# Strassen parts of both feed-forwards: fixed order of TensorE's products, and another order of the downs and of a chunk's last unit

## The chip, the cores and the metric

The kernel runs on one core of a Trainium2 chip. Five engines matter, each with an instruction list of its own that it works through in order, waiting on semaphores: TensorE (PE; its weight loads are listed apart as PEld), VectorE (DVE), ScalarE (ACT), GpSimd (POOL) and SyncE (SP, which only starts transfers). The metric is the device time of one execution in microseconds; the number given is the median of the runs.

## The reference

One decoder layer in float32 over 544 tokens (one prompt of 512 and eight samples of four tokens), width 1024: a feed-forward, a mixing block (RWKV-7 heads beside a short convolution), and a second feed-forward, each with a residual and a layer norm. The change lies in the two feed-forwards alone.

```python
D_MODEL = 1024
D_FF = 2816
...
def swiglu(x, wg, wu, wd):
    return (jax.nn.silu(x @ wg) * (x @ wu)) @ wd
...
    x = layer_norm(ALPHA * x + 0.5 * swiglu(x, p["ffn1_wg"], p["ffn1_wu"], p["ffn1_wd"]), p["ln1_g"], p["ln1_b"])
...
    x = layer_norm(ALPHA * x + 0.5 * swiglu(x, p["ffn2_wg"], p["ffn2_wu"], p["ffn2_wd"]), p["ln3_g"], p["ln3_b"])
```

## The kernel before

**Precision.** Every float32 operand of a product is split into a high and a low part (`split`, `wsplit`: ScalarE copies the high part, VectorE subtracts it for the low one; for weights lines 135 and 136, for others 143 and 144). A block product is three matmuls: high weight times high and low input, low weight times high input (lines 556 to 558).

**Chunks.** The 22 hidden row blocks of 128 are cut into chunks of 4, 4, 4, 4 and 6. For each chunk the kernel computes the hidden rows (`up` in the first chunk, with ordinary products; `pairs` in the others, with Strassen products) and then multiplies them into the output `z` (`downs`, Strassen products, for all chunks but the last, whose ordinary downs follow at the end). The Strassen scheme is Winograd's, with seven products for a two by two split of features and tokens (272 tokens a half).

**Units.** `pairs` works in units, four in a chunk of 4 (gate and up for each pair of rows). A unit is seven products of 12 matmuls, here numbered as they stand for one unit: 1 and 2 (weights part "a"), 3 ("y"), 4 and 5 ("x"), 6 ("b") and 7 ("y"). Products 1, 3, 5 and 6 accumulate in one PSUM bank, `b1`; ScalarE copies the bank out after 1, 3 and 5 (lines 617, 623, 626), and the next accumulation has to wait for the copy. Product 2 has the bank `b4`, products 4 and 7 the bank `b3`. Products 6 and 7 are put off (`tail`) until products 1 and 2 of the next unit have been issued. VectorE adds the copies and banks and multiplies gate and up (lines 583, 584, 593, 599, 603, 619, 627), and `put_h` and `put_b22` make the blocks for the downs out of the hidden rows: B11, NT1 (from the first pair of rows), B21, NT2, T3, T4, B22 (from the second pair), each split into high and low.

**Downs.** `downs` has two groups g of four output blocks, in pairs q = 0 and 1. For each q there are seven products of 6 matmuls. I call them after what they take: m1 (B11), m2 (B21), m5 (NT1), u2 (NT2), u3 (T3), u4 (T4), m3 (B22). m1, u2, u3 and u4 accumulate in one bank (`b1`): m1 is added to `z` by VectorE (line 646) before u2 may go on in the bank, u2 and u3 are copied out by ScalarE (lines 662, 665), u4 is subtracted from `z` (line 646). m2 has a bank `b4` and is added to `z` (line 646). m5 and m3 share a bank `b3`, which VectorE subtracts from u3's copy (line 666) and adds at the end (lines 673 and 676); group 1's results go into `z` by transfers that POOL issues with an accumulating write (line 678). The banks come from two sets, `big` ("mm" in the profile, three banks) and `sm` (five banks).

**Weights.** Each unit and each group of the downs needs four prepared weights, "a", "x", "y" and "b". A counter `self.t` counts products; `plan` sets at which count each part is prepared (`LEAD` products ahead of its unit or group), and `prod` calls `feed`, which issues the preparations that are due: for "a" and "x" a split on ScalarE and VectorE, for "y" two sums on VectorE (lines 521 and 522) and a split, for "b" a half split and then an accumulating transfer issued by POOL. SP loads the raw weights. `hold` remembers the latest operations of an evacuation, and what `put` issues comes on each engine after those.

**Order.** The program is traced whole; then a scheduler at build time, which goes by program order and by its own estimate of when operands are ready, sets the order of each engine's list. It may put a matmul of a later product ahead of one that it thinks would wait. `issue_after` and `after` add edges that bind the order on one engine and cost no instruction.

Of the kernel before, what the change touches and what calls it, by code (L numbers as in the profile page):

```python
# [15 lines left out]
OP = mybir.AluOpType  # L16
# [26 lines left out]
LEAD_B = {0: 25, 1: 23}  # L43
TB = T // 2
HK = KD // 2
# [16 lines left out]
def body(ctx: ExitStack, tc: tile.TileContext, xT, gu1, wd1, win, wo_c, wo_0, wo_1, gu2, wd2, wl, ln3, eye, lora, vec, cst,  # L62
# [260 lines left out]
    class Ffn:  # L323
# [42 lines left out]
        def put_h(self, j, r, parts):  # L366

            hb, (hk, sv) = self.hb, (x[:, r] for x in self.rows)
            lo, hi = slice(0, TB), slice(TB, T)

            def put(v, src):
                split(hb[:, v, 0, r], hb[:, v, 1, r], src)

            for part in parts:
                if j == 0 and part == "lo":
                    put(B11, hk[:, lo])
                elif j == 0:
                    DVE.tensor_tensor(hk[:, lo], hk[:, lo], hk[:, hi], op=OP.subtract)
                    put(NT1, hk[:, lo])
                elif part == "lo":  # L380
                    put(B21, sv[:, lo])
                elif part == "hi":
                    DVE.scalar_tensor_tensor(hk[:, lo], hk[:, lo], -1.0, sv[:, hi], op0=OP.mult, op1=OP.subtract)
                    DVE.tensor_tensor(hk[:, hi], sv[:, hi], hk[:, hi], op=OP.subtract)
                    put(slice(NT2, T3 + 1), hk.rearrange("p (v t) -> p v t", v=2))
                else:
                    DVE.scalar_tensor_tensor(sv[:, lo], hk[:, lo], -1.0, sv[:, lo], op0=OP.mult, op1=OP.subtract)
                    put(T4, sv[:, lo])

        def put_b22(self):  # L390
            split(self.hb[:, B22, 0], self.hb[:, B22, 1], self.rows[1][:, :, TB:])

# [85 lines left out]
        def plan(self):  # L478


            items, t, events = [], 0, []
            for ci, (m0, m1) in enumerate(CHUNKS):
                for key, n in [((ci, "u", u), 7) for u in range(m1 - m0 if ci else 0)] + \
                        [((ci, "d", g), 14) for g in range(2 if ci < LAST else 0)]:
                    items.append(key)
                    lead = dict(LEAD, b=LEAD_B.get(key[2], LEAD["b"] if key[2] == 2 else 15)) if key[1] == "u" else LEAD
                    events += [(t - lead[part], key, part) for part in LEAD]
                    t += n
            events.sort(key=lambda e: e[0])
            return deque((k, p) for k in items for p in "xa"), deque(events)  # L490
# [59 lines left out]
        def prod(self, out, key, part, off, src, first, n=HK):  # L550
            self.feed()
            self.t += 1
            hl = self.w[key, part]
            for i in range(n):
                wh, wl = (hl[:, j, (off + i) * P:(off + i + 1) * P] for j in range(2))
                PE.matmul(out, wh, src(0, i), start=(first and i == 0), stop=False, skip_group_check=True)  # L556
                PE.matmul(out, wh, src(1, i), start=False, stop=False, skip_group_check=True)  # L557
                PE.matmul(out, wl, src(0, i), start=False, stop=(i == n - 1), skip_group_check=True)  # L558
                if i % 2:
                    yield 6 * (TB / 2.4 + 3)  # L560

        def pairs(self, ci):
# [14 lines left out]
            def tail(u, b1, b3, cp):  # L577
                j, i = divmod(u, 2)
                s = self.rows[min(j, 1)]
                if i == 0:  # L580
# [21 lines left out]
                else:  # L602
                    hold(DVE.tensor_tensor(s[:, 0, hi], s[:, 0, hi], cp[:, TB:2 * TB], op=OP.mult))
                    if ci < LAST:
                        self.put_h(j, 0, ("hi", "t4") if j else ("hi",))
                        if j:
                            self.put_b22()
                    else:
                        split(self.hhl[:, 0, 2 * j], self.hhl[:, 1, 2 * j], s[:, 0])

            old = None
            for u in range(m1 - m0):
                a = 0 if u % 2 else 3 * TB
                cp = cpb[:, a:a + 3 * TB]
                b1, b4, b3 = big()[:, :TB], sm()[:, :TB], sm()[:, :TB]
                yield from prod(b1, u, "a", 0, xb(0, 0), True)
                hold(ACT.activation(cp[:, 0:TB], b1, AF.Copy))
                yield from prod(b4, u, "a", HK, xb(HK, 0), True)
                hold(DVE.tensor_tensor(cp[:, 0:TB], cp[:, 0:TB], b4, op=OP.add))
                if old is not None:  # L620
                    yield from old
                yield from prod(b1, u, "y", HK, tb(0), False)
# [5 lines left out]
                old = tail(u, b1, b3, cp)  # L628
            yield from old

        def downs(self, ci):
# [7 lines left out]
            for g in range(2):  # L639
# [8 lines left out]
                def prod(dst, q, part, s, v, first):  # L648
                    off = 2 * q if part == "b" else 4 * q + 2 * s
                    return self.prod(dst[q], key, part, off, blk(v), first, 2)  # L650

                for q in range(2):
                    yield from prod(b1, q, "a", 0, B11, True)
                    add(ds[q], b1[q])
                for q in range(2):
                    yield from prod(b3, q, "x", 1, NT1, True)
                for q in range(2):
                    yield from prod(b4, q, "a", 1, B21, True)
                    add(ds[q], b4[q])
                for q in range(2):  # L660
                    yield from prod(b1, q, "y", 1, NT2, False)
                    hold(ACT.activation(cp[q][:, 0], b1[q], AF.Copy))
                for q in range(2):
# [3 lines left out]
                for q in range(2):  # L667
                    yield from prod(b1, q, "b", 0, T4, False)
                    add(ds[q] + 1, b1[q], OP.subtract)
                for q in range(2):  # L670
# [8 lines left out]

        def main(self):  # L680
            self.open_tv()
            tv = self.inputs()
            self.raw, self.held, self.put_hi, self.t = {}, [], [], 0
# [1095 lines left out]
```

## Time and profile before

| | |
|---|---|
| median of 3 runs | 1071.64 us |
| lowest, highest | 1071.43, 1072.78 us |
| span of the profiled execution | 1069.3 us |
| TensorE's mean granted clock | 0.999 of full speed |

The profile shows one execution: its span goes from the first to the last instruction, and the time of a run has something around it besides (2.3 us between the span and the median). In a list of instructions in order of time the columns are the start in us from the start of the span, the duration in us, the engine, the line of the kernel, the operation, output and inputs by the program's names, shapes, and the count of merged instructions; in brackets stands idle time of the engine before it and what ended it. A matmul's duration is longer than the distance to the next one, since matmuls overlap in the array. In the list of waits the columns are the waiting group, what it waited for, us in total, times, and the longest. In the table by stretches each engine has its busy time and its count of instructions.

The Strassen products run from 53.7 to about 334 us in the first feed-forward and from 742.6 to 1024 us in the second.

### The profile page before, as it was taken

The page shows a single profiled execution, that of the slowest core. Times are in us where ns is not written, and L with a number is a line of the kernel's source. Part 1 is how long each engine was busy: PE and PEld are TensorE (multiplying, and loading weights), DVE is VectorE, ACT ScalarE, POOL GpSimd, SP SyncE. Part 2 cuts the span into 40 slices and gives each one's busy share as a digit, 9 for nine tenths or more (in the row PEclk, how much of TensorE's full clock was granted, in tenths as well). Part 3 has the DMA queues.
Part 4 walks back from the last instruction along what each step waited for, and adds up shares of the span by engine and source line. Part 5 has one row for each costly group of instructions (what it writes and reads, how often), then busy time and mean ns, then how long its engine had stood idle before and what let it go on. Part 6 is the DMA issues. An engine that isn't in the chain of part 4 may idle for free.

```text
span 1069.3 us, 22615 instructions
## 1 busy us (share of the span) xinstructions
PE 1050.8 (98%) x9178; PEld 1010.5 (95%) x9178; DVE 844.6 (79%) x1557; ACT 582.9 (55%) x1070; POOL 155.3 (15%) x273
## 2 busy tenths in 40 slices
PE   9999999999999999999999999999999999999997
PEld 8999999999999999899889988999999999999996
DVE  6797888979875777794578658888979888797657
ACT  5746465555553668654344435767555555655524
POOL 0121121211200032133101200001211212111000
PEclk9999999999999999999999999999999999999999
DMA  8558585676754223324145624334766948568512
GB/s 296 128 116 186 124 191 137 149 169 136 183 118 158 79 92 105 85 82 99 41 143 163 172 81 149 132 119 79 156 162 137 199 103 197 141 136 189 147 43 84
DMA packets 91528, 144.48 MB, mean 135 GB/s; under 512 B 34848, under 2 KB 52384, under 8 KB 91296
## 3 DMA queue, kind: packets, MB, share of 16 engines
q1 hardware_dynamic: 68144, 110.76, 33.7%
q0 software_dynamic: 22848, 31.72, 19.4%
q8 instruction: 72, 1.18, 0.4%
q10 hardware_dynamic: 432, 0.56, 0.2%
q14 instruction: 32, 0.26, 0.1%
HBM read 128.81 MB, written 9.75 MB: 130 GB/s over the span
## 4 chain that ended last, share of the span: by engine, by line
PE 77%; DVE 13%; ACT 6%; issue 2%; DMA 1%; POOL 0%; ACTq 0%; DVEq 0%; SPq 0%
PE mm L556 9%; PE mm L557 9%; PE mm L558 9%; PE mm L155 6%; PE sm L556 6%; PE sm L557 6%; PE sm L558 6%; PE mm L156 6%; PE mm L157 6%; DVE hhl L144 2%; DVE hl L136 2%; PE sm L444 1%; PE sm L1169 1%; ACT hl L135 1%; PE mm L787 1%
## 5 line engine op out<-in xcount | busy, mean ns | idle before, releaser
L136 DVE TENSOR_TENSOR hl<-raw,hl 128x1024 fp32r<-128x1024 f32 (+3 forms) x230 | 269.8, 1177 | 61.4 <-ACT hl L135 60.2
L135 ACT ACTIVATE hl<-raw 128x1024 fp32r<-128x1024 f32 (+3 forms) x230 | 232.8, 1020 | 67.3 <-DVE raw L522 43.5
L155 PE MATMUL mm<-xhl,hl 128*128 128x256 f32 (+1 forms) x704 | 208.9, 298 | 0.5 <-ACT xhl L143 0.5
L156 PE MATMUL mm<-xhl,hl 128*128 128x256 f32 (+1 forms) x704 | 203.0, 289 | 0.4 <-DVE xhl L144 0.4
L157 PE MATMUL mm<-xhl,hl 128*128 128x256 f32 (+1 forms) x704 | 202.0, 287 | 0.0
L155 PEld LDWEIGHTS mm<-xhl,hl 128*128 128x128 f32 x704 | 132.0, 188 | 6.7 <-issue 1.8
L156 PEld LDWEIGHTS mm<-xhl,hl 128*128 128x128 f32 x704 | 132.3, 188 | 2.4 <-DVE xhl L144 0.8
L157 PEld LDWEIGHTS mm<-xhl,hl 128*128 128x128 f32 x704 | 132.3, 188 | 0.3 <-issue 0.2
L558 PE MATMUL sm<-xhl,hl 128*128 128x272 f32 x432 | 125.2, 290 | 0.0
L557 PE MATMUL sm<-xhl,hl 128*128 128x272 f32 x432 | 124.4, 288 | 0.0
L556 PE MATMUL sm<-xhl,hl 128*128 128x272 f32 x432 | 124.1, 287 | 0.0
L556 PE MATMUL mm<-tv,hl 128*128 128x272 f32 x288 | 83.4, 290 | 0.3
L558 PE MATMUL mm<-tv,hl 128*128 128x272 f32 x288 | 83.4, 290 | 0.0
L557 PE MATMUL mm<-tv,hl 128*128 128x272 f32 x288 | 83.0, 288 | 0.0
L556 PEld LDWEIGHTS sm<-xhl,hl 128*128 128x128 f32 x432 | 81.3, 188 | 0.0
L557 PEld LDWEIGHTS sm<-xhl,hl 128*128 128x128 f32 x432 | 81.3, 188 | 0.0
L558 PEld LDWEIGHTS sm<-xhl,hl 128*128 128x128 f32 x432 | 81.3, 188 | 0.0
L535 POOL DMA_DIRECT2D raw<-in_wd x32 | 39.2, 1462 | 287.8 <-DVE hlb L144 225.2
L529 POOL DMA_DIRECT2D raw<-in_gu x36 | 43.3, 1203 | 203.0 <-DVE hlb L144 137.6
L557 PE MATMUL mm<-hhl,hl 128*128 128x272 f32 x192 | 56.0, 291 | 0.8 <-DVE hhl L144 0.2
L556 PE MATMUL mm<-hhl,hl 128*128 128x272 f32 x192 | 56.3, 299 | 0.3
L556 PEld LDWEIGHTS mm<-tv,hl 128*128 128x128 f32 x288 | 54.2, 188 | 1.9 <-ACT cpb L623 1.9
(421 smaller groups left out, 2713.5 us busy)
## 6 DMA issues: line engine op xcount, KB each, us to landing
raw<-in_gu SPq DMA_DIRECT2D x84, 512.0 KB, 4.4
raw<-in_gu POOLq DMA_DIRECT2D x36, 512.0 KB, 7.0
raw<-in_wd SPq DMA_DIRECT2D x32, 512.0 KB, 4.5
raw<-in_win SPq DMA_DIRECT2D x26, 512.0 KB, 3.6
raw<-in_wd POOLq DMA_DIRECT2D x32, 256.0 KB, 5.7
z<-sv POOLq DMA_DIRECT2D x16, 272.0 KB, 8.2
raw<-in_wo_c SPq DMA_DIRECT2D x8, 512.0 KB, 3.6
raw<-in_wd SPq DMA_DIRECT2D x8, 384.0 KB, 3.1
```

What stands on the lines that cost most here:

```text
L135: seen["hi"] = ACT.activation(hl[:, 0, a:b], raw[:, a:b], AF.Copy)
L136: seen["lo"] = DVE.tensor_tensor(hl[:, 1, a:b], raw[:, a:b], hl[:, 0, a:b].bitcast(F32), op=OP.subtract)
L144: return DVE.tensor_tensor(lo, x, hi.bitcast(F32), op=OP.subtract)
L155: PE.matmul(out, wh, src[:, 0, k, c0:c1], start=(start and i == 0), stop=False)
L156: PE.matmul(out, wh, src[:, 1, k, c0:c1], start=False, stop=False)
L157: seen["fill"] = PE.matmul(out, wl, src[:, 0, k, c0:c1], start=False, stop=(stop and i == n - 1))
L444: PE.matmul(o[i][h][:, :c1 - c0], block(hl, v, k), xhl[:, y, k, c0:c1], start=(k == 0 and j == 0), stop=(k == KD - 1 and j == 2), skip_gro ...
L529: POOL.dma_start(x.rearrange("p (s c) -> p s c", s=2), bass.AP(tensor=a11.tensor, offset=a11.offset, ap=[[2 * D, P], [P * 2 * D, 2], [1, 5 ...
L535: POOL.dma_start(four(x)[:, i], bass.AP(tensor=a11.tensor, offset=a11.offset, ap=[[DFF, P], [P * DFF, 2], [1, 256]]), accum_op=OP.add)
L556: PE.matmul(out, wh, src(0, i), start=(first and i == 0), stop=False, skip_group_check=True)
L557: PE.matmul(out, wh, src(1, i), start=False, stop=False, skip_group_check=True)
L558: PE.matmul(out, wl, src(0, i), start=False, stop=(i == n - 1), skip_group_check=True)
```

## The change

`prod` gets an edge: the first matmul of every Strassen product comes after the last matmul of the product before it in program order. So TensorE works through these products in the order in which the program has them.

In `pairs`, the last unit of a chunk issues its product 2 (`second`) after product 5 and ahead of its own 6; products 6 and 7 of the unit before follow directly upon product 1.

In `downs`, the order is by hand. Before, each group went m1, m5, m2, u2, u3, u4, m3, each for q = 0 and 1. After, group 0 goes m1(0), m1(1), m5(0), m5(1), m2(0), u2(0), u2(1), m2(1), u3(0), u3(1); then m1(0) of group 1; then group 0's u4(0), u4(1), m3(0), m3(1); then group 1's m1(1), m5(0), m5(1), u2(0), u2(1), m2(0), u3(0), u3(1), m2(1), u4(0), u4(1), m3(0), m3(1). u2 takes its second block of K first.

The low part of B22 comes on VectorE after the low part of T4, and group 1's weights "a" are prepared 12 products ahead instead of 9.

```diff
+LEAD_A = 12
...
-                    lead = dict(LEAD, b=LEAD_B.get(key[2], LEAD["b"] if key[2] == 2 else 15)) if key[1] == "u" else LEAD
+                    if key[1] == "u":
+                        lead = dict(LEAD, b=LEAD_B.get(key[2], LEAD["b"] if key[2] == 2 else 15))
+                    else:
+                        lead = dict(LEAD, a=LEAD_A) if key[2] else LEAD
...
-                self.put_b22()
+                self.put_b22(self.lo)
...
+        def put_b22(self, prev=None):
+            with ExitStack() as st:
+                if prev is not None:
+                    st.enter_context(tc.issue_after(prev.ins))
+                split(self.hb[:, B22, 0], self.hb[:, B22, 1], self.rows[1][:, :, TB:])
...
-        def prod(self, out, key, part, off, src, first, n=HK):
+        def prod(self, out, key, part, off, src, first, ks=range(HK)):
             self.feed()
             self.t += 1
             hl = self.w[key, part]
-            for i in range(n):
+            for n, i in enumerate(ks):
                 wh, wl = (hl[:, j, (off + i) * P:(off + i + 1) * P] for j in range(2))
-                PE.matmul(out, wh, src(0, i), start=(first and i == 0), stop=False, skip_group_check=True)
+                e = PE.matmul(out, wh, src(0, i), start=(first and n == 0), stop=False, skip_group_check=True)
+                if n == 0 and self.pe is not None:
+                    after(e, self.pe)
                 PE.matmul(out, wh, src(1, i), start=False, stop=False, skip_group_check=True)
-                PE.matmul(out, wl, src(0, i), start=False, stop=(i == n - 1), skip_group_check=True)
+                self.pe = PE.matmul(out, wl, src(0, i), start=False, stop=(n == len(ks) - 1), skip_group_check=True)
...
+            def second(u, cp):
+                b4 = sm()[:, :TB]
+                yield from prod(b4, u, "a", HK, xb(HK, 0), True)
+                hold(DVE.tensor_tensor(cp[:, 0:TB], cp[:, 0:TB], b4, op=OP.add))
...
                 yield from prod(b1, u, "a", 0, xb(0, 0), True)
                 hold(ACT.activation(cp[:, 0:TB], b1, AF.Copy))
-                yield from prod(b4, u, "a", HK, xb(HK, 0), True)
-                hold(DVE.tensor_tensor(cp[:, 0:TB], cp[:, 0:TB], b4, op=OP.add))
+                if not last:
+                    yield from second(u, cp)
                 if old is not None:
                     yield from old
...
-                old = tail(u, b1, b3, cp)
+                old = tail(u, b1, b3, cp, partial(second, u, cp) if last else tuple)
...
+            m1, m2, m3, m5, u2, u3, u4 = group(0)
+            for f, q in ((m1, 0), (m1, 1), (m5, 0), (m5, 1), (m2, 0), (u2, 0), (u2, 1), (m2, 1), (u3, 0), (u3, 1)):
+                yield from f(q)
+            rest = (u4, 0), (u4, 1), (m3, 0), (m3, 1)
+            m1, m2, m3, m5, u2, u3, u4 = group(1)
+            yield from m1(0)
+            for f, q in rest + ((m1, 1), (m5, 0), (m5, 1), (u2, 0), (u2, 1), (m2, 0), (u3, 0), (u3, 1), (m2, 1),
+                                (u4, 0), (u4, 1), (m3, 0), (m3, 1)):
+                yield from f(q)
```

More of the change, by code (lines that the diff above doesn't have):

```diff
@@ L575, in pairs, with tail @@
             lo, hi = slice(0, TB), slice(TB, T)
-            def tail(u, b1, b3, cp):
+            def tail(u, b1, b3, cp, between):
                 j, i = divmod(u, 2)
                 s = self.rows[min(j, 1)]
+                yield from between()
                 if i == 0:
@@ L637, in blk, with group @@
                 return lambda j, i: hb[:, v, j, i, :]
-            for g in range(2):
+            def group(g):
                 key = (ci, "d", g)
@@ L666, in downs, with u4, m3 @@
                          DVE.tensor_tensor(cp[q][:, 1], cp[q][:, 1], b3[q], op=OP.subtract))
-                for q in range(2):
+                def u4(q):
                     yield from prod(b1, q, "b", 0, T4, False)
                     add(ds[q] + 1, b1[q], OP.subtract)
-                for q in range(2):
+                def m3(q):
                     zh = z[:, ds[q]:ds[q] + 2, TB:]
@@ L682, in main @@
             tv = self.inputs()
-            self.raw, self.held, self.put_hi, self.t = {}, [], [], 0
+            self.raw, self.held, self.put_hi, self.t, self.pe, self.lo = {}, [], [], 0, None, None
             self.todo, self.events = self.plan()
```

29 lines of the change are left out of this document (15 added, 14 removed).

## The prediction

> **What bounds the kernel now.** I read the page first, then the weight loads' waits, then a table by stretches, then VectorE's list through one change from unit products to down products.
>
> ```profile
> span 1069.3 us, 22615 instructions
> PE 1050.8 (98%) x9178; PEld 1010.5 (95%) x9178; DVE 844.6 (79%) x1557; ACT 582.9 (55%) x1070; POOL 155.3 (15%) x273
> ...
> PE 77%; DVE 13%; ACT 6%; issue 2%; DMA 1%; POOL 0%; ACTq 0%; DVEq 0%; SPq 0%
> ```
>
> ```profile
> PEld mm L557 <- DVE hhl L144: 2.3, 7, 0.4
> PEld mm L556 <- ACT sv L662: 2.0, 8, 0.3
> PEld mm L556 <- ACT cpb L623: 1.9, 7, 0.3
> ...
> PEld mm L556 <- ACT cpb L626: 1.4, 7, 0.2
> ```
>
> TensorE is the bound at first sight, and 13% of the ending chain lies on VectorE. The weight loads of Strassen products wait in four kinds of place, 7 or 8 times each: once per chunk. The change aims at these.
>
> ```profile
> core 0: us, PE busy (x) PEld busy (x) DVE busy (x) ACT busy (x) POOL busy (x), PEclk, DMA share, GB/s
> 118.20:136.10 17.90, 17.79 (x140) 17.37 (x138) 17.67 (x37) 8.31 (x15) 2.41 (x2) 1.00 0.64 127
> 146.20:168.70 22.50, 22.50 (x181) 22.50 (x181) 17.05 (x29) 12.95 (x22) 3.64 (x3) 1.00 0.82 179
> ```
>
> In unit products (146 to 169) VectorE is busy 17.05 of 22.5 us. In down products (118 to 136) it is busy 17.67 of 17.90: there two engines are full, and that decides what an order of TensorE is worth.
>
> ```profile
> 118.04 0.29 PE L558 MATMUL sm<-xhl,hl 128*128 128x272 f32 x1
> ...
> 122.40 0.79 PE L557 MATMUL mm<-hhl,hl 128*128 128x272 f32 x2
> ...
> 147.58 0.28 PE L556 MATMUL mm<-xhl,hl 128*128 128x272 f32 x1
> ...
> 168.68 0.28 PE L556 MATMUL mm<-xhl,hl 128*128 128x272 f32 x1
> ...
> 182.87 0.29 PE L558 MATMUL sm<-xhl,hl 128*128 128x272 f32 x1
> ```
>
> Between 147.58 and 168.68 lie 14 products of 12 matmuls without a wait: 21.10/168 = 0.1256 us each, so a unit product takes 1.507 us and a down product of six 0.754. The last matmul of a chunk's unit products comes at 118.04 and, a chunk later, at 182.87: a period of 64.83 us. It holds 336 matmuls of units and 168 of downs, 63.30 us by that pitch. **So 1.53 us of each steady chunk is waiting**, and six transitions are steady (three in each feed-forward).
>
> **What the change removes, adds and moves.** The edges cost no instruction; nothing is computed more or less. They remove cases where one matmul was slipped in front of a wait, as here:
>
> ```profile
> 145.64 0.29 PE L558 MATMUL sm<-xhl,hl 128*128 128x272 f32 x1
> 145.97 0.39 PE L556 MATMUL mm<-tv,hl 128*128 128x272 f32 x1
> 146.20 0.29 PE L557 MATMUL mm<-tv,hl 128*128 128x272 f32 x1
> ```
>
> A matmul of the unit's fifth product was put after only four of the fourth, and waits for the copy of L623: 0.33 + 0.23 us where 0.25 belong, 0.31 lost. In order, eight more matmuls (1.0 us) lie before it and the wait is gone. Likewise moving the last unit's second product behind its fifth puts 1.5 us over L626. The downs' copies L662 and L665 (0.39 us) get one or two products, 0.75 to 1.5 us, over them; the second product of u2 starts with the half of K that is ready earlier. Inside the pair units I cost all this at a full gain. The earlier sixth product of the unit before has one product in front of its copy instead of two, 1.5 us against 0.4, which I take as cover; a 1.05 us weight split in front of the copy would leave nearly none.
>
> Now what is late next. Call T0 the start of a chunk's first down product that follows the units (118.17 here, 0.13 after 118.04). TensorE accumulates u2 of group 1 into the bank in which m1 of group 1 lies, so u2(1) waits for the add of m1(1) into z, the sixteenth down product's L646. Before, seven products stand from that u2(1) to the end of the downs. After, nine do: m2 has gone behind u2, and u2(1) is product 20 of 28, due 19 x 0.754 = 14.3 us after T0. VectorE's run up to that add:
>
> ```profile
> 117.59 0.72 DVE L144 TENSOR_TENSOR hhl<-hk,hhl 128x544 fp32r<-128x544 f32 x1 [0.29 <-ACT hhl L143]
> ...
> 118.58 0.43 DVE L599 TENSOR_TENSOR cpb<-cpb,sm 128x272 f32<-128x272 f32 x1
> 118.93 0.43 DVE L387 SCALAR_TENSOR_TENSOR sv<-hk,sv 128x272 f32<-128x272 f32 x1
> ...
> 131.30 0.68 DVE L144 TENSOR_TENSOR hlb<-raw,hlb 128x512 fp32r<-128x512 f32 x1
> ...
> 132.25 0.72 DVE L673 TENSOR_TENSOR z<-z,cpb 128x544 f32<-128x544 f32 x1
> 132.88 0.43 DVE L646 TENSOR_TENSOR z<-z,mm 128x272 f32<-128x272 f32 x1
> 133.23 0.43 DVE L676 TENSOR_TENSOR z<-z,sm 128x272 f32<-128x272 f32 x1
> 133.58 0.43 DVE L646 TENSOR_TENSOR z<-z,mm 128x272 f32<-128x272 f32 x1
> ...
> 136.07 1.22 DVE L136 TENSOR_TENSOR hl<-raw,hl 128x1024 fp32r<-128x1024 f32 x1 [0.23 <-ACT hl L135]
> ```
>
> From 117.59 to 136.07 no row shows idle time before it. The add of m1(1) is the row at 133.58 and ends at 134.01, **15.84 us after T0: 1.5 later than the new order asks for it.** The operations ahead of it are the same set before and after: the program puts five weight splits and the first group's adds before it in both (counters 30 to 40 of the plan; LEAD_A only brings one of them from 33 to 30). The last unit's second product adds two small operations at 0.35 us of pitch (118.58 to 118.93) nearer to T0; in exchange P7 of the unit before ends 0.75 us sooner and with it the weight sums L521 and L522 start sooner. I take that as even. The held-back B22 split only changes places within the run; its user m3 is product 14 of the new order, 9.8 us after T0. SP's loads and POOL's accumulating transfers follow the same splits; LEAD_A's part issues none.
>
> One place I expect to gain: the row at 132.88 shows an add pass L676, which has to follow L673 on the same tile. In the new order the first such add is long done there, so the second one can take its place, 0.35 us earlier (134.01 to 133.66). Bounds: 0 to 0.96 (if the split at 131.30, 0.61 of pitch, is passed too); I take 0.35, the nearer row.
>
> Behind the waiting u2(1) on TensorE stands all that is left of the downs and the next chunk; ScalarE's copies L662 and L665 wait for it in turn, with a product or more between each copy and its reader as above. A wait on TensorE costs what the rows at 145.97 and 146.20 show after L623: 0.06 from the end of the awaited operation and 0.10 at the next matmul. The sum for a **steady chunk**: add done at T0 + 15.49; 0.16; nine down products and 28 unit products, 390 x 0.1256 = 48.98. Period 64.63 against 64.83: **-0.20, six times, -1.2 us.**
>
> The two first chunks, which follow the ordinary `up` products:
>
> ```profile
> 53.73 0.29 PE L556 MATMUL mm<-hhl,hl 128*128 128x272 f32 x1
> ...
> 71.23 0.28 PE L556 MATMUL mm<-xhl,hl 128*128 128x272 f32 x1
> ...
> 75.35 0.29 PE L558 MATMUL sm<-hhl,hl 128*128 128x272 f32 x1
> ```
>
> ```profile
> 68.38 0.43 DVE L646 TENSOR_TENSOR z<-z,mm 128x272 f32<-128x272 f32 x1
> ...
> 758.58 0.43 DVE L646 TENSOR_TENSOR z<-z,mm 128x272 f32<-128x272 f32 x1
> ```
>
> ```profile
> 757.82 0.29 PE L556 MATMUL mm<-xhl,hl 128*128 128x272 f32 x1
> ...
> 761.20 0.28 PE L558 MATMUL mm<-xhl,hl 128*128 128x272 f32 x1
> ...
> 765.26 0.29 PE L558 MATMUL sm<-hhl,hl 128*128 128x272 f32 x1
> ```
>
> First feed-forward: the add would end at 68.81 - 0.35 = 68.46, plus 0.16 and 54 x 0.1256 = 6.78 gives 75.40. Before, the downs ended at 75.48 with two matmuls of the next chunk already done (from 71.23), so 75.23: +0.17. Second: 758.66 + 6.94 = 765.60 against 765.38 less four such matmuls (757.82 to 761.20), 764.88: +0.72, less the 0.31 at the next unit's fifth product, +0.41. These early matmuls are the cover that the edges take away.
>
> ```profile
> 330.46 0.27 PE L156 MATMUL mm<-hhl,hl 128*128 128x256 f32 x1
> ...
> 330.87 0.28 PE L557 MATMUL mm<-tv,hlb 128*128 128x272 f32 x1
> ```
>
> ```profile
> 1020.47 0.29 PE L751 MATMUL sm<-hhl,hl 128*128 128x288 f32 x1
> ...
> 1020.95 0.29 PE L557 MATMUL mm<-tv,hlb 128*128 128x272 f32 x1
> ```
>
> The last chunks' last unit: 0.41 and 0.48 where two matmuls take 0.25: -0.16 and -0.23. Sum: -1.2 + 0.17 + 0.41 - 0.39 = -1.0 us. The profiled execution spans 1069.3 us, the median of the runs is 2.3 above; both fall alike, to 1068.3 and **1070.6 us, no change** that a measurement tells (0.2%, 2.1 us, is about what it can).
>
> **The rivals.** *TensorE alone binds*: VectorE's adds come in time, every wait goes. Six times 1.53, 75.23 - 53.73 - 21.10 = 0.40, 764.88 + 0.31 - 742.63 - 21.10 = 1.46 and 0.39: 11.4 us less, 1060.2.
>
> ```profile
> 742.63 0.29 PE L556 MATMUL mm<-hhl,hl 128*128 128x272 f32 x1
> ```
>
> For it speaks 95% of weight loads; against it VectorE's 17.67 of 17.90. The Trainium skill, Perfetto Trace Analysis, Identifying the Most-Contended Engine, would have the engine with the highest occupancy optimized first, judging TensorE by its weight loads; by that rule it is TensorE throughout, and this rival follows. The same page's Optimization Strategy says that the contended engine can change over time; this trace's downs agree with that, at 98.7% VectorE. Chance 0.12.
>
> *The add comes earlier than I think*: it passes the split at 131.30 too, 0.61 in each of eight transitions, 4.9 us more: 1065.7. For it speaks that VectorE's list is no strict program order (132.88 before 133.23); against it that everything ahead is ready by then. Chance 0.18.
>
> *VectorE's run gets holes*: slower. The order fixed, VectorE waits for ScalarE between the last blocks of h (as at 117.59, 0.29 idle) and the add passes nothing (0.35): 0.64 in each of eight transitions, +5.1, 1075.7. It ends slower than before by what can be told once the average is over (2.1 + 1.0)/8 = 0.4 us each. For it: nine products behind the gate, no early matmuls to fill it; against: 18 us without a hole before. Chance 0.24.
>
> *It doesn't do what it says* (the scheduler had nearly this order inside the units anyway): no change; within the forecast.
>
> **Chances.** Forecast, with the last rival, 0.46. Faster 0.30 (0.12 + 0.18), same 0.46, slower 0.24. The range 1064.5 to 1076 takes in the second and third rivals' times and leaves out most of the first. The likeliest case alone: 1069.5 to 1073.7.
>
> **What would show it.** One wait of about 1.2 us on TensorE per chunk at u2(1) of group 1, released by L646; no idle before VectorE's rows in the downs; no waits left on L623, L626, L662; chunk period near 64.6. Wrong if that wait is missing or the period is near 63.3, or if VectorE's rows in the downs show idle time and the period passes 65.2.

## The result and the profile after

The changed kernel takes 1078.0 us (median of 5 runs, 1077.2 to 1079.3), the kernel before, on the same chip, 1071.5 (5 runs). The ratio is 1.0058, with a 95% interval of 1.0047 to 1.0068: **slower by 6.5 us**, where 1.0 us less was forecast. The page of the changed kernel answers to the lines shown of before:

```profile
span 1075.5 us, 22603 instructions
...
PE 1045.4 (97%) x9178; PEld 1008.5 (94%) x9178; DVE 846.6 (79%) x1557; ACT 586.9 (55%) x1070; POOL 156.0 (15%) x273
...
PE 68%; DVE 19%; ACT 7%; issue 4%; DMA 1%; POOL 0%; ACTq 0%; DVEq 0%; SPq 0%
```

No engine has more than a few us more to do. But VectorE's share of the chain that ends last has grown from 13 to 19%, and TensorE's has fallen from 77 to 68%. The list of the weight loads' waits says where (in the changed kernel the three matmuls of a block stand in L563, L566, L567; the add into `z` in L663; the low half of a split in L145):

```profile
PEld mm L563 <- DVE z L663: 11.9, 9, 1.5
PEld mm L566 <- DVE hhl L145: 4.2, 7, 0.7
```

The waits of before on the copies L623, L626 and L662 are gone, as planned. In their place stands one wait of up to 1.5 us, nine times, for an add into `z`, and the wait for a low half (L145, L144 before) has grown from 2.3 to 4.2 us. TensorE's list through a steady chunk, in order of time:

```profile
118.69 0.29 PE L567 MATMUL sm<-xhl,hl 128*128 128x272 f32 x1
118.82 0.28 PE L563 MATMUL mm<-hhl,hl 128*128 128x272 f32 x1
...
135.35 0.39 PE L563 MATMUL mm<-hhl,hl 128*128 128x272 f32 x1 [1.30 <-DVE z L663]
135.58 0.29 PE L566 MATMUL mm<-hhl,hl 128*128 128x272 f32 x1
...
184.24 0.29 PE L567 MATMUL sm<-xhl,hl 128*128 128x272 f32 x1
```

The row at 135.35 is u2(1) of group 1, the gate that the prediction named, released by the very add that it named. It starts 1.47 us later than the pitch asks, and the matmul after it loses another 0.10. The period of a steady chunk, from the last matmul of its units to that of the next one's, is 184.24 - 118.69 = 65.55 us, against 64.83 before and 64.63 forecast; the prediction named a period above 65.2 as a sign of being wrong. VectorE's list from T0 = 118.82 to that add:

```profile
118.59 0.73 DVE L145 TENSOR_TENSOR hhl<-hk,hhl 128x544 fp32r<-128x544 f32 x1
119.23 0.44 DVE L145 TENSOR_TENSOR hhl<-sv,hhl 128x272 fp32r<-128x272 f32 x1
119.59 0.43 DVE L609 TENSOR_TENSOR cpb<-cpb,sm 128x272 f32<-128x272 f32 x1
...
122.39 0.43 DVE L663 TENSOR_TENSOR z<-z,mm 128x272 f32<-128x272 f32 x1
122.85 0.72 DVE L145 TENSOR_TENSOR hhl<-hk,hhl 128x544 fp32r<-128x544 f32 x1
123.50 1.07 DVE L145 TENSOR_TENSOR hhl<-sv,hhl 128x272 fp32r<-128x272 f32 x2
...
129.95 1.12 DVE L663 TENSOR_TENSOR z<-z,mm 128x272 f32<-128x272 f32 x3
131.16 1.23 DVE L137 TENSOR_TENSOR hl<-raw,hl 128x1024 fp32r<-128x1024 f32 x1
...
132.90 1.35 DVE L696 TENSOR_TENSOR z<-z,cpb 128x544 f32<-128x544 f32 x2
134.17 0.78 DVE L699 TENSOR_TENSOR z<-z,sm 128x272 f32<-128x272 f32 x2
134.87 0.43 DVE L663 TENSOR_TENSOR z<-z,mm 128x272 f32<-128x272 f32 x1
```

The add ends at 135.30, **16.48 us after T0, where 15.49 was forecast** and 15.84 stood before. The same 31 operations lie in the run from L609 (L599 before) to the add in both kernels. The 0.99 us has three parts:

- The run begins later: L609 starts at T0 + 0.77; L599 before at 118.58, T0 + 0.41. That is 0.36.
- The add passes nothing: group 0's four sums (L696, L696, L699, L699; L673 and L676 before) all stand ahead of it. The forecast had it pass the last, 0.35.
- The run is longer, 135.30 - 119.59 = 15.71 against 134.01 - 118.58 = 15.43: 0.28 of holes. Rows follow each other at 0.35 us for a small operation; from 122.39 to 122.85 it is 0.46, and the three adds from 129.95 to 131.16 take 1.21 for 1.05.

Both holes wait for ScalarE, whose list has the high halves that these two low halves are subtracted from: one ends at 122.82, the other at 131.12.

```profile
122.16 0.66 ACT L144 ACTIVATE hhl<-hk 128x544 fp32r<-128x544 f32 x1 [0.74 <-DVE hk L385]
...
130.06 1.06 ACT L136 ACTIVATE hl<-raw 128x1024 fp32r<-128x1024 f32 x1 [2.49 <-DVE raw L529]
```

Both come of the new order of VectorE's own work. Before, the low half of B22 (the 544 columns from `sv`) stood right ahead of the low half from `hk`:

```profile
121.39 0.72 DVE L144 TENSOR_TENSOR hhl<-sv,hhl 128x544 fp32r<-128x544 f32 x1
122.03 0.72 DVE L144 TENSOR_TENSOR hhl<-hk,hhl 128x544 fp32r<-128x544 f32 x1
```

The change holds it back, into the merged row at 123.50, and its 0.64 us of pitch no longer fills the time in which ScalarE makes the high half. At the second place, before, two adds and a sum (L673) filled the 1.33 us from 128.83 to 130.16; now three adds fill 1.05. No run gives the old order back at these two places alone.

Over the whole span, 6.2 us longer: six periods at +0.72 make 4.3; the chunks ahead of the first steady transition take 0.26 and 0.39 more; the last chunks, beyond their transition, 0.01 and 0.10 less; from the last Strassen product to the end it is 0.48 more; the Strassen parts begin 0.39 later, and the stretch between them is 0.48 longer. These make 6.2.

### The profile page after: what moved, and what is told of

Its sections match the earlier page's. It is cut to its first block, busy times and chain, and to the rows that moved or that the text cites. A ratio compares the mean times of both kernels' runs of the same rounds, so it can differ in the third digit from the quotient of the medians.

```text
span 1075.5 us, 22603 instructions
## 1 busy us (share of the span) xinstructions
PE 1045.4 (97%) x9178; PEld 1008.5 (94%) x9178; DVE 846.6 (79%) x1557; ACT 586.9 (55%) x1070; POOL 156.0 (15%) x273
## 4 chain that ended last, share of the span: by engine, by line
PE 68%; DVE 19%; ACT 7%; issue 4%; DMA 1%; POOL 0%; ACTq 0%; DVEq 0%; SPq 0%
PE mm L563 7%; PE mm L567 7%; PE mm L566 7%; PE mm L156 6%; PE mm L157 6%; PE mm L158 6%; PE sm L567 5%; PE sm L566 5%; PE sm L563 5%; DVE hl L137 3%; ACT hl L136 3%; DVE hhl L145 2%; PE sm L448 1%; PE sm L1204 1%; PE mm L822 1%
## 5 line engine op out<-in xcount | busy, mean ns | idle before, releaser
L137 DVE TENSOR_TENSOR hl<-raw,hl 128x1024 fp32r<-128x1024 f32 (+3 forms) x230 | 270.0, 1178 | 70.7 <-ACT hl L136 68.4
L567 PE MATMUL sm<-xhl,hl 128*128 128x272 f32 x432 | 125.3, 290 | 0.0
L566 PE MATMUL sm<-xhl,hl 128*128 128x272 f32 x432 | 124.4, 288 | 0.0
L563 PE MATMUL sm<-xhl,hl 128*128 128x272 f32 x432 | 124.1, 287 | 0.0
L567 PE MATMUL mm<-tv,hl 128*128 128x272 f32 x288 | 83.4, 289 | 0.0
L566 PE MATMUL mm<-tv,hl 128*128 128x272 f32 x288 | 83.1, 289 | 0.0
L563 PE MATMUL mm<-tv,hl 128*128 128x272 f32 x288 | 82.8, 287 | 0.0
L563 PEld LDWEIGHTS sm<-xhl,hl 128*128 128x128 f32 x432 | 81.3, 188 | 0.0
L566 PEld LDWEIGHTS sm<-xhl,hl 128*128 128x128 f32 x432 | 81.3, 188 | 0.0
L567 PEld LDWEIGHTS sm<-xhl,hl 128*128 128x128 f32 x432 | 81.3, 188 | 0.0
L563 PE MATMUL mm<-hhl,hl 128*128 128x272 f32 x192 | 57.1, 297 | 9.9 <-DVE z L663 9.9
L566 PE MATMUL mm<-hhl,hl 128*128 128x272 f32 x192 | 55.8, 291 | 2.7 <-DVE hhl L145 2.7
L567 PE MATMUL sm<-hhl,hl 128*128 128x272 f32 x192 | 55.3, 288 | 0.0
```

The costliest lines, as they stand in the source:

```text
L137: seen["lo"] = DVE.tensor_tensor(hl[:, 1, a:b], raw[:, a:b], hl[:, 0, a:b].bitcast(F32), op=OP.subtract)
L563: e = PE.matmul(out, wh, src(0, i), start=(first and n == 0), stop=False, skip_group_check=True)
L567: self.pe = PE.matmul(out, wl, src(0, i), start=False, stop=(n == len(ks) - 1), skip_group_check=True)
```

## The experiments

All times are medians; each ratio is against the kernel before on the same chip. "Period" is that of the first steady chunk, read as above. "Add" is the end of the add of m1(1) of group 1, counted from T0. In the lists below the line numbers of kernels that have one line more in `plan` are higher by one (L564 for L563, L664 for L663).

| kernel | time, us | ratio [95%] | period, us | add, us |
|---|---|---|---|---|
| before | 1071.5 | 1 | 64.83 | 15.84 |
| changed | 1078.0 | 1.0058 [1.0047, 1.0068] | 65.55 | 16.48 |
| e1_edges_only | 1073.55 | 1.0015 [1.0005, 1.0024] | 65.10 | 15.84 |
| e2_order_only | 1083.69 | 1.0114 [1.0086, 1.0142] | 65.31 | 16.48 |
| e3_sums_later | 1072.44 | 1.0009 [1.0000, 1.0019] | 64.78 | 14.51 |
| e4_second_as_before | 1081.39 | 1.0091 [1.0076, 1.0106] | 65.98 | 16.12 |
| e5_copy_first | 1067.02 | 0.9955 [0.9942, 0.9967] | 64.02 | 14.52 |
| e6_cover_u2 | 1066.60 | 0.9955 [0.9942, 0.9967] | 63.95 | 14.50 |
| f0_copy_first_alone | 1077.76 | 1.0058 [1.0042, 1.0073] | 65.53 | 16.47 |
| f1_half_dose | 1067.53 | 0.9960 [0.9947, 0.9974] | 64.22 | 15.14 |
| f2_gate_later | 1078.69 | 1.0060 [1.0045, 1.0074] | 65.57 | 16.49 |
| f3_gate_later_copy_first | 1073.48 | 1.0014 [1.0004, 1.0024] | 64.92 | 16.48 |
| e7_cover_both | 1070.37 | 0.9982 [0.9973, 0.9991] | 64.52 | 14.52 |
| e8_gate_later | 1067.62 | 0.9961 [0.9947, 0.9975] | 64.17 | 14.53 |

Theory G says that the add of m1(1) of group 1 is a gate, and that the time follows its place and what TensorE has to do behind it. The rivals are given with each run.

### The two halves of the change: e1 and e2

e1 is the kernel before with the edges alone, e2 the changed kernel without them.

```diff
# e1, on the kernel before
-                PE.matmul(out, wh, src(0, i), start=(first and i == 0), stop=False, skip_group_check=True)
+                e = PE.matmul(out, wh, src(0, i), start=(first and i == 0), stop=False, skip_group_check=True)
+                if i == 0 and self.pe is not None:
+                    after(e, self.pe)
...
# e2, on the changed kernel
-                if n == 0 and self.pe is not None:
-                    after(e, self.pe)
```

> The edges alone, on the old order of downs and units. Theory G (the gate: u2(1) of group 1 waits for VectorE's run up to the add of m1(1)): in the old order that u2(1) is product 22, due 21 x 0.754 = 15.8 us after the downs' start, and the add was done at 15.84, so the gate hardly binds: 1070 to 1074 us. Theory F (the fixed order itself costs, since it takes away the early matmuls that filled waits): most of the loss of 6.5 us is here, 1076 to 1078.

> The changed kernel without the edges: the scheduler may move matmuls again. G: the wait for the add stays and is filled by some four early matmuls per chunk at most (0.5 us x 8): 1073 to 1076. F: all of the loss goes, 1071.5 or less.

The weight loads' waits of e1 (L628 is the copy after a unit's product 5, L664 that after u2):

```profile
PEld mm L556 <- ACT cpb L628: 4.4, 7, 0.7
...
PEld mm L556 <- ACT sv L664: 3.5, 8, 0.4
PEld mm L556 <- ACT cpb L664: 3.1, 8, 0.5
```

and of e2 (L638 is the copy after a unit's product 3):

```profile
PEld mm L563 <- ACT cpb L638: 12.4, 15, 2.8
```

In e1 the gate doesn't bind. TensorE simply waits where before it had work to slip in: the last unit's product 6 waits 0.64 + 0.10 us for its copy (1.4 us over 7 waits in the list of before), and u3 for the copy after u2. So the edges alone cost 2 us. e1 came out where G had it. e2 missed both theories: without the edges the new order costs 5.7 us more than with them, since the scheduler puts other matmuls ahead and the accumulation waits for the copy of product 3, 15 times, up to 2.8 us. (The table's 65.31 us is e2's first steady chunk, with 0.59 us of this; a later one takes 66.92.) The loss is therefore not in the edges by themselves. They help this order and hurt the old one. Nor do the edges delay the add: it ends at T0 + 15.84 in e1, with edges and the old order, and at T0 + 16.48 in e2, with the new order and no edges. Its lateness belongs to the new order.

### The gate: e3 and e4

e3 moves group 0's four sums behind the add of m1(1) of group 1, on VectorE alone; TensorE's order stays.

```diff
                 def m3(q):
-                    zh = z[:, ds[q]:ds[q] + 2, TB:]
-                    if g == 0:
-                        DVE.tensor_tensor(zh, zh, cp[q], op=OP.add)
                     yield from prod(b3, q, "y", 0, B22, False)
+                    if g:
+                        sums(q)
+
+                def sums(q):
+                    zh = z[:, ds[q]:ds[q] + 2, TB:]
+                    if g == 0:
+                        DVE.tensor_tensor(zh, zh, cp[q], op=OP.add)
                     dst = cp[q][:, 0] if g else zh[:, 0]
                     hold(DVE.tensor_tensor(dst, dst, b3[q], op=OP.add))
...
-            for f, q in rest + ((m1, 1), (m5, 0), ...
+            for f, q in rest + ((m1, 1),):
+                yield from f(q)
+            for q in range(2):
+                sums(q)
+            for f, q in ((m5, 0), ...
```

> The changed kernel with group 0's last sums (two of 0.63 and two of 0.35 us of VectorE's pitch, 1.96 us) moved behind the add of m1(1) of group 1. G: the add ends 1.96 us earlier, the wait of 1.47 at u2(1) goes nearly, some 1.3 us in each of eight transitions: 1066 to 1069, faster than before. F, and any theory in which VectorE's order does not matter: 1077 to 1079.

VectorE's list in e3, the waits of its weight loads, and ScalarE's list at the start of the next chunk:

```profile
131.89 0.69 DVE L145 TENSOR_TENSOR hlb<-raw,hlb 128x512 fp32r<-128x512 f32 x1
132.49 0.43 DVE L663 TENSOR_TENSOR z<-z,mm 128x272 f32<-128x272 f32 x1
132.84 1.35 DVE L701 TENSOR_TENSOR z<-z,cpb 128x544 f32<-128x544 f32 x2
```

```profile
PEld mm L563 <- ACT cpb L633: 6.0, 8, 0.8
PEld mm L566 <- DVE hhl L145: 4.2, 7, 0.7
```

```profile
140.10 1.06 ACT L136 ACTIVATE hl<-raw 128x1024 fp32r<-128x1024 f32 x1 [3.02 <-DVE raw L529]
141.07 0.61 ACT L144 ACTIVATE hlb<-raw 128x512 fp32r<-128x512 f32 x1
141.59 1.99 ACT L136 ACTIVATE hl<-raw 128x1024 fp32r<-128x1024 f32 x2
143.48 0.38 ACT L633 ACTIVATE cpb<-mm 128x272 f32<-128x272 f32 x1
```

The add stands ahead of the sums, 1.97 us earlier, and the wait at u2(1) is gone. The time falls by 5.6 us, but not to the 1066 to 1069 expected, for **a second gate stood right behind the first**: the copy L633 after a chunk's very first product waits on ScalarE behind four high halves of weight splits, and the chunk's third product waits 0.69 + 0.10 us for it. In the changed kernel TensorE came there too late to notice.

e4 puts the last unit's second product back where it was.

```diff
-                last = u == m1 - m0 - 1
+                last = False
```

> The changed kernel with the last unit's second product where it was. Theory H (bringing that product's two VectorE operations to the end of the units is what cost): 1072 to 1074. G: VectorE's run starts about 0.36 us sooner and the wait of 0.25 at the unit's sixth product comes back: within 1 us of the changed kernel, 1077 to 1079.

The weight loads' waits of e4:

```profile
PEld mm L563 <- DVE z L663: 11.9, 9, 1.5
PEld mm L563 <- ACT cpb L643: 4.4, 7, 0.7
...
PEld mm L566 <- DVE hhl L145: 2.4, 7, 0.7
```

Slower by 3.4 us than the changed kernel, more than any theory had: product 6 waits 0.65 + 0.10 us again, as in e1, since with the edges nothing slips in. Yet the add comes at T0 + 16.12, 0.36 earlier. That is the first part of the 0.99 us, tested by itself: the late second product holds the run up by 0.36. TensorE's wait at u2(0) shrinks by 0.35 too, so the gate's wait looks unchanged.

### The second gate, and the dose: e5, f0, f1

e5 is e3 with the second unit's part "x" split one product later, so that the copy L633 comes ahead of that split's high half. f0 is the changed kernel with this step alone; f1 is e5 with only q = 1's two sums moved.

```diff
# e5, f0, f1
                         lead = dict(LEAD, b=LEAD_B.get(key[2], LEAD["b"] if key[2] == 2 else 15))
+                        lead["x"] -= key[2] == 1
# f1, on e5
-                    if g:
+                    if g or q == 0:
                         sums(q)
...
-            for q in range(2):
-                sums(q)
+            sums(1)
```

> e3_sums_later with one more step: in plan() the split of the second unit's part x comes one product later, so that ScalarE's copy of a chunk's very first product (L633 in e3) is issued before that split's high half and not behind it. In e3 TensorE waits 0.69 + 0.10 us there in each of eight chunks (ACT cpb L633: 6.0 us over 8 waits). Theory G (VectorE's add of m1(1) of group 1 was the gate in the changed kernel, and moving the sums behind it only handed the time on to this copy): the wait at the third product of a chunk's first unit falls under 0.2 us, the steady period from 64.78 to about 64.1, and the time from 1072.4 to 1066 - 1068. Rival T (the time of e3 isn't set by single waits but by VectorE's whole load in a chunk: whatever wait is taken away comes back at the next product that needs VectorE): the period stays above 64.6 and the time at 1071 - 1074.

> The changed kernel with only the later split of the second unit's part x; group 0's sums stay ahead of the add of m1(1) of group 1. Theory G: the gate of 1.47 us at u2(1) of group 1 stands where it was, and as the changed kernel has no wait at the copy of a chunk's first product, nothing is to be had: 1077 - 1079.5. Rival T: the same within 1 us. It is the zero dose for f1_half_dose.

> Half the dose of e5_copy_first: of group 0's four sums only the two of q = 1 stand behind the add of m1(1) of group 1; those of q = 0 stay ahead of it. Theory G: VectorE reaches the add about 1.0 us earlier than in the changed kernel (two ops of 0.64 and 0.38 us, 0.35 of pitch less), so the wait at u2(1) of group 1 falls from 1.47 to 0.4 - 0.6 us, and the time lies between f0 and e5: 1070 - 1073. Rival T: within 1 us of e3 and e5 alike, or of f0.

The weight loads' waits of f0, the zero dose:

```profile
PEld mm L564 <- DVE z L664: 11.9, 9, 1.5
```

of f1, half of it:

```profile
PEld mm L564 <- DVE z L664: 1.6, 7, 0.4
```

of e5, all of it (the wait for `z` that is left is the first chunk's of the second feed-forward):

```profile
PEld mm L567 <- DVE hhl L145: 4.2, 7, 0.7
...
PEld mm L564 <- ACT cpb L641: 0.4, 1, 0.4
PEld mm L564 <- DVE z L664: 0.4, 1, 0.4
```

and ScalarE's list in e5, in which the copy (now L634) has moved ahead of one split:

```profile
141.10 1.04 ACT L136 ACTIVATE hl<-raw 128x1024 fp32r<-128x1024 f32 x1
142.05 0.38 ACT L634 ACTIVATE cpb<-mm 128x272 f32<-128x272 f32 x1
142.33 1.05 ACT L136 ACTIVATE hl<-raw 128x1024 fp32r<-128x1024 f32 x1
```

The later split alone gains nothing (f0), as G had it. The sums alone (e3) gain 5.6, both together 11.0 from the changed kernel, into the range expected: e5 beats the kernel before by 0.45%. Half the dose gave nearly all of it, 1067.5, below the 1070 to 1073 that G named: the add at T0 + 15.14 is only 0.13 + 0.11 us late, because the wait at u2(0) of group 0 brings TensorE to the gate 0.67 us later, and one at m1(1) another 0.18, which I hadn't counted.

### The gate moved on TensorE: f2 and f3

f2 leaves VectorE alone and puts a product more ahead of the gate; f3 adds the later split.

```diff
# f2 and f3, on the changed kernel (group 1)
-            ... (u2, 0), (u2, 1), (m2, 0), (u3, 0), (u3, 1), (m2, 1),
+            ... (u2, 0), (m2, 0), (u2, 1), (u3, 0), (m2, 1), (u3, 1),
# f3 besides
+                        lead["x"] -= key[2] == 1
```

> The changed kernel with one step on TensorE alone: in group 1 the product m2(0) stands ahead of u2(1), and m2(1) ahead of u3(1); VectorE's sums stay where they are. Theory G (the time of the changed kernel is set by VectorE's add of m1(1) of group 1, at T0 + 16.47, followed by what TensorE still has to do behind it): one down product of 0.754 us fewer stands behind the gate, so the wait of 1.47 us falls to about 0.72, the steady period from 65.55 to about 64.8, and the time by eight times 0.75, to 1071 - 1073. Rival F (VectorE's whole run through the downs is the bound, its gate only the place where that is seen): VectorE still ends its run where it did, the wait comes back at a later product, and the time stays at 1076.5 - 1079.

> f2_gate_later with the later split of the second unit's part x (the step that took e3 to e5). In f2 the gate's wait halved (0.71 us) and a wait of 0.54 + 0.10 us came at the third product of a chunk's first unit, for ScalarE's copy L633, behind two high halves of weight splits. Theory G (f2's gain was real and handed on to that copy, as in e3): the copy's wait goes under 0.2, the gate's stays near 0.7, the period falls from 65.57 to 64.8 - 65.0 and the time to 1072 - 1075. Rival F (VectorE's whole run is the bound, whatever wait shows it): the wait comes back at a later product, period above 65.4, 1077 - 1079.5.

The waits of f2:

```profile
PEld mm L563 <- DVE z L663: 5.9, 9, 0.8
PEld mm L563 <- ACT cpb L633: 4.6, 8, 0.6
```

and of f3:

```profile
PEld mm L564 <- DVE z L664: 5.9, 9, 0.8
```

f2 alone speaks for the rival: the gate's wait halved and the time stayed, at 1078.7. But the wait that came instead is the copy L633 again, and f3, which takes that away, falls to 1073.5, where G had it. So for the changed kernel the rival's "VectorE's whole run is the bound" falls: the wait did not come back a second time.

### The wait at u2(0), and three orders that gave nothing more: e6, e7, e8

e6 is e5 with m2(1) ahead of u2(0) in group 0; e7 is e6 with m1(0) of group 1 ahead of group 0's u3 and with f2's order; e8 is e6 with f2's order alone.

```diff
# e6, on e5 (group 0)
-            ... (m2, 0), (u2, 0), (u2, 1), (m2, 1), (u3, 0), (u3, 1)):
+            ... (m2, 0), (m2, 1), (u2, 0), (u2, 1), (u3, 0), (u3, 1)):
# e7, on e6: group 0's u3 behind group 1's m1(0), and f2's order
-            ... (u2, 0), (u2, 1), (u3, 0), (u3, 1)):
+            ... (u2, 0), (u2, 1)):
                 yield from f(q)
+            first = (u3, 0), (u3, 1)
...
-            for f, q in rest + ((m1, 1),):
+            for f, q in first + rest + ((m1, 1),):
```

> e5_copy_first with one more step: in group 0 the product m2(1) stands ahead of u2(0), so that u2(0), which waits 0.58 + 0.10 us for the last low half of the second factor's split in the changed kernel and in e3, is due one down product (0.754 us) later. Theory G: that wait falls from about 0.68 us to under 0.1 in each of the transitions (six or seven of them), which brings the gate at u2(1) of group 1 nearer by as much (in e3 it had some 0.2 to 0.8 us of room), so 0.2 to 0.6 us a transition are left: 1062.5 - 1066.5. Rival T: 1071 - 1074, the wait back at a later product.

> e6_cover_u2, in which TensorE still waits at u3(0) of group 0 for ScalarE's copy (L683, 0.38 + 0.11 us) and at u2(1) of group 1 for the add (L664, 0.25 + 0.10), with a product put over each: m1(0) of group 1 stands ahead of u3(0) of group 0, and m2(0) of group 1 ahead of its u2(1). Theory G: both waits go but for about 0.1, the period falls from 63.96 to 63.3 - 63.5 (63.30 is 504 matmuls at the pitch), the time to 1061.5 - 1064.5. Rival F: the waits come back at later products, period above 63.8, time 1065.5 - 1068.

> e6_cover_u2 with the step of f2 alone: in group 1 m2(0) stands ahead of u2(1) and m2(1) ahead of u3(1). e6 waits at two places in a steady chunk, 0.38 + 0.11 us at u3(0) of group 0 and 0.25 + 0.10 at u2(1) of group 1. Theory G: the second goes, the first stays, period from 63.96 to 63.55 - 63.7, time from 1066.6 to 1063 - 1065.5. Rival F (each product put over a wait makes another come late, as m1(0) did in e7, whose weight split was not ready): the period stays at 63.9 or above, time 1066 - 1069.

The waits of e6 (L683 is the copy after u2):

```profile
PEld mm L564 <- ACT cpb L683: 3.0, 7, 0.4
PEld mm L564 <- DVE z L664: 2.2, 7, 0.4
```

and of e7:

```profile
PEld mm L568 <- DVE hl L137: 4.6, 6, 0.8
...
PEld sm L564 <- DVE cpb L688: 2.2, 13, 0.2
...
PEld mm L564 <- DVE z L664: 0.4, 1, 0.4
```

In e6 the wait at u2(0) is gone, and its 0.67 us is handed on: 0.37 + 0.11 at u3(0), which now follows u2(0) with one product between instead of two, and 0.24 + 0.10 at m1(1) of group 1. That last product starts 11.96 us after T0 in the changed kernel, 11.97 in e5, 11.95 in e6 and 11.98 in e8, whatever waits stand ahead of it. In each case the second of the three adds that in the changed kernel begin at 129.95 has, by the pitch of 0.35, ended 0.05 to 0.06 us before, so this product too is held by VectorE's run. Period and time are those of e5; G's 1062.5 to 1066.5 was missed, if only by 0.1 us. e7 covers the copy and finds that the weights of m1(0), now two products earlier, aren't split in time (L137): 0.70 + 0.10 us. Two further waits of 0.23 and 0.19 us stand at group 0's m3, for the subtraction L688. With the 63.30 us of matmuls these make the period of 64.52, slower than e6. e8 rested on a misreading of mine: the wait at 129.94 in e6 is the sixteenth down product, m1(1) of group 1 (T0 = 117.99, 15 products of 0.754 and the 0.48 at u3(0) make 129.8), which waits for a bank, and not u2(1). Moving a product behind it could not help, and the period rose by 0.22 us. In e6, e7 and e8, then, G's forecasts all failed, and what their rivals said, that a wait taken away comes back at another product, is what the lists show; e8's period and time lie where its rival had them. G is shown for the step from the changed kernel to e5, and not for a step beyond it. The lowest time found is 1066.6 to 1067.0, e5 or e6.

## Why the prediction was wrong

**The bound was named rightly.** The prediction said that u2(1) of group 1 would wait for the add, once per chunk, and that the waits on L623, L626 and L662 would go. All of that is in the profile after. Its formula for a steady chunk holds as well: the add's place after T0, 0.16, and the matmuls behind it at 0.1256 us. With the measured places it gives 16.48 + 0.16 + 48.98 = 65.62 for the changed kernel (65.55 measured), 15.14 + 49.14 = 64.28 for f1 (64.22), 16.12 + 49.14 + 0.75 for product 6 = 66.01 for e4 (65.98), and with six matmuls fewer 16.48 + 0.16 + 48.23 = 64.87 for f3 (64.92). For e5 it gives 63.66, below the 64.02 measured: there the add no longer binds. The matmuls' 63.30, the 0.67 at u2(0) and the 0.16 at m1(1) of group 1 make 64.13, 0.11 too much.

**The step that failed is the term "add done at T0 + 15.49".** It came at 16.48, and 0.99 us too late makes the period 0.92 longer than forecast (65.55 against 64.63). Of its three parts:

- "I take that as even", of the last unit's late second product: it isn't. The run starts 0.36 us later, and e4 takes all of it away. What was to balance it was mis-sized too: the unit before ends its product 7 a whole unit product sooner, 1.51 us at the pitch, where the prediction has 0.75, and even that did not make it even.
- "the second one can take its place, 0.35 earlier": the add passed no sum. That rested on one row in which an add stood ahead of a sum in another order of the program; in the new program the sums of group 0 precede the add, and VectorE's list followed. e3 and f1 move them by hand, and the time follows.
- no holes in VectorE's run: 0.28 us of them, at the places shown above, read from the trace alone. "The held-back B22 split only changes places within the run" put at nothing what opened the first of them. No run takes just these away.

The rival "VectorE's run gets holes and the add passes nothing" had two of the three, and its size for them, 0.64 a transition, is what was measured (0.28 + 0.35). One of the two holes lies where it said, between the last blocks of h, the other at a weight split; but they come of the new order, not of its being fixed (e2). The late second product, 0.36 in each of eight transitions, would make 1078.6 of its 1075.7; measured is 1078.0. Its chance of 0.24 was too low, for it speaks of the very term on which the sum hung, with three assumptions on the good side.

**Cover.** The forecast took the downs to be covered and left the wait at u2(0) out. It is 0.57 + 0.10 us in the changed kernel, more than the 0.27, 0.10 and 0.08 lost there before. In the changed kernel it costs nothing, as the gate lies behind it; in e5 it is most of the waiting that is left, though taking it away by itself gained nothing (e6).

**First chunks**: +0.26 and +0.39, against +0.17 and +0.41 forecast, but only because errors cancel, which is luck. The add came too late here as well, 15.55 and 16.83 us after the first down product where the forecast had 14.73 and 16.03. Against that, the wait for L626 in the chunk's last unit, which went, was left out (0.24 and 0.25). And four matmuls that the forecast did not see in the old order lay ahead of its last unit's product 6, and so ahead of 118.04:

```profile
114.39 0.29 PE L556 MATMUL mm<-hhl,hl 128*128 128x272 f32 x1
```

They are the first of the next down product, from 114.39 to 114.77, so that the T0 of before starts with its fifth matmul. In order they follow the units, and the first chunk ends 0.50 us sooner by that alone. The sums are 0.17 + 0.82 - 0.24 - 0.50 = 0.25 and 0.41 + 0.80 - 0.25 - 0.50 = 0.46. In the steady chunks the four stand at both ends of a period and change nothing. **Last units**: -0.39 was forecast from two matmuls that took 0.41 and 0.48 us; measured are -0.01 and -0.10, and +0.48 behind them in the second feed-forward. Before, the stretch at the second place held other work, as its TensorE list shows, which stands next to the row at 1020.47 shown in the prediction:

```profile
1020.07 0.56 PE L751 MATMUL mm<-hhl,hl 128*128 128x288 f32 x3
```

These four matmuls of the closing downs now come after the last Strassen product (L786 at 1029.56 in the changed kernel), so what looked like a wait was partly work that had to be done anyway. In e1 and e4, which keep the last unit as before, the stretch from the last Strassen product to the end is 45.5 us, in the changed kernel 46.1.

**The other rivals.** "TensorE alone binds" (1060.2) is refuted by this change: its waits for copies went and the time rose. The Trainium skill, Perfetto Trace Analysis, Identifying the Most-Contended Engine, would have had TensorE optimized first, as the engine with the highest occupancy; by the 94% of the weight loads it still is that engine, and the time was set on VectorE at one add. "The add comes earlier than I think" fell with the row at 134.87.

**What stays open.** The Strassen parts begin 0.4 to 1.1 us later than before in every kernel tried, at rows whose code none of them changes. The stretch between the two feed-forwards, also unchanged, lasts 409.0 to 413.2 us over the profiled executions, so single spans are no measure of a gain below some 4 us; the periods and the medians are. That VectorE's holes would be gone by themselves with an earlier high half on ScalarE wasn't tried. B22's place, group 1's earlier weights "a" and the turned order of K in u2 were not taken away singly, and what bounds e5 and e6, 0.7 us a chunk above the matmuls' 63.30, is not shown.

## What to carry to other kernels

Fixing the order of one engine takes away the work that its scheduler slipped into waits, so each covered wait has to be paid by the order itself; and where another engine is full, read off what stands ahead of the one operation that the new order awaits, and move it behind in the program, since here the list did not reorder it. When a wait is removed and the time doesn't move (f2), look at which wait is next on the same engine before calling it a throughput bound: two waits may cover each other, and only taking away both shows what either costs. In a sum that hangs on one operation's arrival, three small favourable assumptions are one large one.

## What the runs showed of the hardware that was not expected

A hole on VectorE costs more than the idle time that the list shows. Small operations that wait for nothing start every 0.35 us though each lasts 0.43. Ahead of the changed kernel's row at 122.85 the idle time is 0.03 us, too short to be shown in brackets, yet the distance from the start before is 0.46: 0.11 is lost, the overlap of 0.08 included. Ahead of the row at 131.16 it is 0.09 and 0.16. So a run without a bracket isn't yet a run without holes.
